# Attention stage: sample values of two pages ahead of the 256-column scores, and the head norm's small VectorE work behind a block's softmax difference

## Chip, cores and metric

One NeuronCore of one Trainium2 chip. The metric is the device time of the whole program in microseconds (us), the median of three runs. "TensorE" is PE in the profile (PEld is its weight load), VectorE is DVE, ScalarE is ACT, GpSimd is POOL, SyncE is SP.

## What is computed

One inference step of a two-layer decoder, all in float32: a Conformer-convolution layer and a differential-attention layer, each with a SwiGLU FFN behind it. The change lies in the attention layer, for 512 prompt tokens and 8 samples of 8 new tokens with 512 cached keys and values in 4 pages each; there are 8 heads.

```python
def diff_weights(scores, q_pos, k_pos, rel_bias, lam):
...
    logits = jnp.where((dist >= 0)[None, None, None], logits, -jnp.inf)
    p = jax.nn.softmax(logits, axis=-1)
    return p[:, :, 0] - lam * p[:, :, 1]
...
def attn_out(o, g, w, lam_init):
    B, T = o.shape[0], o.shape[1]
    o = rms_norm(o, g) * (1.0 - lam_init)
    return o.reshape(B, T, V_WIDTH) @ w
```

`o` is, for each head, the difference of two softmaxes times the values; it is RMS-normed over the head's 128 values ("head norm" below).

## The kernel before

Everything but attention is matmuls with split float32 operands. Attention is written as closures that are put into a plan by `at(round, rank, f)`; `play` runs the rounds in order and the closures of a round by rank. Each engine's instructions stand in the order in which they are written (class `InOrder`), so the plan sets the order on every engine's queue.

Each head takes four rounds. `prompt` handles its four blocks of 128 query rows as (3), (2) and (1, 0): `scores` (TensorE into the two banks `bS`, then on VectorE a custom bias-and-max instruction for each of the two softmaxes, and the exponentials with their sums on ScalarE), one round later `differ` (VectorE: RECIPROCAL, TENSOR_SCALAR and SCALAR_TENSOR_TENSOR, which waits for the sums of the exponentials) and `turn` (TensorE transposes, from the tile `pt`), and then `values`. Block (2) has score rows of 384 columns, blocks (1, 0) of 256 and 128.

`prompt_out` is the head norm: `squares`, then `power`, which on VectorE takes a RECIPROCAL and a TENSOR_REDUCE (the sums of squares), two TENSOR_TENSOR and a TENSOR_SCALAR on 128x4 elements, and on GpSimd raises four columns to the power -0.5 (the pow instruction, `sm<-sm,mhalf 128x4`). `scale` follows on VectorE: one 128x4 TENSOR_TENSOR that reads the result of pow, and the 128x512 multiplication into `t`; then `turn` and `low`. For head h the stages `scores` of the next head's block (2) and `power` stand in the same round.

`prepare_low` has GpSimd make the low parts of the queries and keys of a later head: two 128x512 subtractions, `whi<-xlo,whi` and `wlo<-xhi,wlo`, which wait for two casts of `prepare` on ScalarE. On GpSimd's queue they stand directly behind the pow of a head. The last two rounds with the norm of head 6 have no `prepare_low`; there `w_o_weights` has GpSimd make the low parts of the output projection's weights (`wlo<-raw,whi`) instead.

`sample` does the same for one sample and all heads: `scores` (q against the pages, `raw,qz`), `exponent`, `norm` and `combine`, `values` (32-column matmuls `raw,aTs` for pages 0 to 3 and `vv,aTs` for the new tokens), `power`, `scale`, `turn`. Near the end of attention `early` fills TensorE with the first matmuls of the output projection.

Of the kernel before, what the change touches and what calls it, by code (L numbers as in the profile page):

```python
# [36 lines left out]
def build(tc, A, O):  # L37
# [3 lines left out]
    with ctx:  # L41
# [35 lines left out]
        def tt():  # L77
            return tmp.tile([128, 640], F32, name="t")

        def sm(n=8):  # L80
            t = small.tile([128, 16], F32, name="sm")
            return t[:, :n]
# [195 lines left out]
        class Factors:  # L278
# [7 lines left out]
            def sums(self, i):  # L286
                return self.thi[:, i], self.tlo[:, i]
# [324 lines left out]
        with tc.tile_pool(name="h0", bufs=1) as hp0:  # L612
# [29 lines left out]
            with tc.tile_pool(name="cv", bufs=1) as cvp:  # L642
                c = cvp.tile([128, KT, T], F32, name="c")
                smid = Stats()
                with tc.tile_pool(name="u", bufs=2) as up:
# [146 lines left out]
                    r = smid.tok_half(0)  # L792
# [18 lines left out]
                    for i, (k, hf) in enumerate(steps):  # L811
# [5 lines left out]
                        if i == 0:  # L817
                            r = smid.tok_half(1)
# [38 lines left out]
        with tc.tile_pool(name="kvq", bufs=1) as kp:  # L857
# [164 lines left out]
            with tc.tile_pool(name="att", bufs=2) as ap_:  # L1022
                pages, slots = {}, {}

                def load_pages(src, b):
                    t = wp.tile([128, 4096], F32, name="raw", bufs=2)
                    for j in range(4):
                        if (b, j) not in slots:
                            slots[b, j] = nc.sync.value_load(pt[0:1, 4 * b + j:4 * b + j + 1], min_val=0, max_val=39)
                        r = slots[b, j]  # L1030
                        nc.sync.dma_start(out=t[:, j * 1024:(j + 1) * 1024],
                                          in_=A[src][bass.ds(r, 1)].rearrange("o p n -> p (o n)"))
                    pages[src, b] = t.rearrange("p (j h n) -> p j h n", j=4, h=8)
# [4 lines left out]
                def next_turn():  # L1038
                    turns[0] += 1
                    return bT[turns[0] % 2]  # L1040
# [4 lines left out]
                def at(r, rank, f):  # L1045
                    plan.setdefault(r, []).append((rank, f))

                def sample(b, r):
                    st_ = {}
# [45 lines left out]
                    def pov():  # L1095
                        return bP[:, :256].rearrange("p (g e) -> p g e", g=2)

                    def values(ks):
                        V, aT = pages["cv", b], st_["aT"]
                        for k in ks:  # L1100
                            for j in range(4):
                                if k < 4:
                                    l, r_ = aT[:, k, 16 * j:16 * j + 32], V[:, k, 2 * j:2 * j + 2, :]
                                else:
                                    l = aT[:64, k, 16 * j:16 * j + 32]
                                    r_ = vv[:64, 4, 256 * j:256 * j + 256].rearrange("p (g e) -> p g e", g=2)
                                pe.matmul(pov()[32 * j:32 * j + 32], lhsT=l, rhs=r_, start=(k == 0), stop=(k == 4))
                        if 4 in ks:
                            if b < 7:
                                load_pages("cv", b + 1)  # L1110
                            sq = st_["sq"] = tt()
                            ac.activation(out=sq[:, :256], in_=bP[:, :256], func=AF.Square)
# [37 lines left out]
                    at(r + 1, 0.2, norm)  # L1150
                    at(r + 1, 4, combine)
                    at(r + 2, 4, lambda: values((0, 1)))
                    at(r + 3, 2.47, lambda: values((2, 3, 4)))
                    at(r + 4, 1.9, power)
                    at(r + 5, 0.1, scale)
                    at(r + 5, 2.2, turn)
# [89 lines left out]
                def prompt_out(X, r):  # L1246
                    st_ = {}


                    def squares():  # L1250
                        pr = next_turn()[:, :4]
                        pe.matmul(pr, lhsT=rev, rhs=X.s0[:, :4], start=True, stop=True)
                        sq = st_["sq"] = tt()
                        ac.activation(out=sq[:, :512], in_=X.po, func=AF.Square)
                        st_["pr"] = pr

                    def power():
                        ss, r0 = sm(), sm()
                        st_["r0"] = r0
                        ve.reciprocal(out=r0[:, :4], in_=st_["pr"])  # L1260
                        ve.tensor_reduce(out=ss[:, :4], in_=st_["sq"][:, :512].rearrange("p (i e) -> p i e", i=4),
                                         axis=AX.X, op=ALU.add)
                        ve.tensor_tensor(out=ss[:, :4], in0=ss[:, :4], in1=r0[:, :4], op=ALU.mult)
                        ve.tensor_tensor(out=ss[:, :4], in0=ss[:, :4], in1=r0[:, :4], op=ALU.mult)
                        ve.tensor_scalar(out=ss[:, 4:8], in0=ss[:, :4], scalar1=1.0 / 128, scalar2=EPS,
                                         op0=ALU.mult, op1=ALU.add)
                        sc = st_["sc"] = sm()
                        po_.tensor_tensor(out=sc[:, :4], in0=ss[:, 4:8], in1=mhalf[:, :4], op=ALU.pow)

                    def scale():  # L1270
                        sc, r0 = st_["sc"], st_["r0"]
                        ve.tensor_tensor(out=sc[:, 4:8], in0=sc[:, :4], in1=r0[:, :4], op=ALU.mult)
                        on = st_["on"] = tt()
                        ve.tensor_tensor(
                            out=on[:, :512].rearrange("p (i e) -> p i e", i=4),
                            in0=X.po.rearrange("p (i e) -> p i e", i=4),
                            in1=sc[:, 4:8].rearrange("p (i o) -> p i o", o=1).broadcast_to([128, 4, 128]),
                            op=ALU.mult)

                    def turn():  # L1280
                        pT = X.po
                        for i in range(4):
                            pe.transpose(out=pT[:, i * 128:(i + 1) * 128], in_=st_["on"][:, i * 128:(i + 1) * 128],
                                         identity=ident)
                        ac.activation(out=xhi[:, X.h, :TP], in_=pT, func=AF.Copy, scale=gsub)

                    def low():
                        ve.scalar_tensor_tensor(out=xlo[:, X.h, :TP], in0=X.po, scalar=gsub,
                                                in1=xhi[:, X.h, :TP].bitcast(F32), op0=ALU.mult, op1=ALU.subtract)

                    at(r, 6, squares)
                    at(r + 1, 2.5, power)
                    q = 0 if X.last else 1
                    at(r + 1 + q, 2.3 if q else 7, scale)
                    at(r + 2 + q, 2.48 if q else 5, turn)
                    at(*((r + 4, 2.5) if q else (r + 2, 6)), low)


                for h_ in range(H):
                    X = Head()  # L1300
                    X.last = h_ == H - 1
                    r = 4 * h_ + 1
                    sample(h_, r - 1)
                    at(max(r - 3, 0), 6 if h_ else 0, lambda X=X, h_=h_: prepare(X, h_))
                    at(max(r - 1, 0), 0.1, lambda X=X: prepare_low(X))
                    prompt(X, (3,), r)
                    prompt(X, (2,), r + 1)
                    prompt(X, (1, 0), r + 2)
                    prompt_out(X, r + 4)
# [197 lines left out]
```

## Time and profile before

| | us |
|---|---|
| median of 3 runs | 1344.92 (1343.82 to 1345.35) |
| the profiled execution's own time | 1345.44 |
| its span, first to last instruction | 1343.7 |
| PE busy | 1327.9 (99%) |
| DVE busy | 918.1 (68%) |
| ACT busy | 599.2 (45%) |
| POOL busy | 117.9 (9%) |

Busy times count an instruction from its start to its end; PE's ends are modelled, so a busy PE can hold waits. All instructions of the kernel carry one line, L62, because a helper issues them; groups are told apart by the tiles. The attention stage lies from about 784 to 901 us, and repeats every 13.6 us, once for each head.

### The profile page before, as it was taken

How to read it: one execution, taken by the hardware profiler on the slowest of the kernel's cores; microseconds unless marked ns; L12 is line 12 of the kernel's file. 1: busy time of each engine (PE TensorE's matmuls, PEld its weight loads, DVE VectorE, ACT ScalarE, POOL GpSimd, SP SyncE). 2: the span in 40 equal slices, each digit the busy share in tenths (PEclk: the TensorE clock that was granted, in tenths of full speed). 3: DMA queues.
4: the chain of work that ended last, by engine and by line, in shares of the span. 5: the costliest groups of instructions: out<-in, count | busy, mean ns of one | idle time of the engine just before them, and what ended most of it. 6: DMA issues, size and time to landing. Idle time of an engine off the chain costs nothing.

```text
span 1343.7 us, 25259 instructions
## 1 busy us (share of the span) xinstructions
PE 1327.9 (99%) x10320; PEld 1225.1 (91%) x10320; DVE 918.1 (68%) x1803; ACT 599.2 (45%) x1224; POOL 117.9 (9%) x112
## 2 busy tenths in 40 slices
PE   8999999999999999999999999999999999999998
PEld 7988499999999999998787766689999999999998
DVE  6999375798658747764555258876679856865862
ACT  5122363345525524543454357764435533543550
POOL 0001112000000000011223113232100000000000
PEclk9999999999999999999999999999999999999999
DMA  8655412131321231252224178964021331231121
GB/s 307 203 170 167 108 66 93 32 126 64 123 98 64 95 126 64 88 208 91 79 98 160 63 267 322 343 232 156 32 94 64 110 111 63 105 116 63 63 95 71
DMA packets 57398, 168.00 MB, mean 125 GB/s; under 512 B 5970, under 2 KB 12754, under 8 KB 57154
## 3 DMA queue, kind: packets, MB, share of 16 engines
q1 hardware_dynamic: 55552, 163.85, 34.9%
q10 hardware_dynamic: 1730, 2.54, 0.6%
q8 instruction: 81, 1.33, 0.4%
q14 instruction: 35, 0.29, 0.1%
HBM read 145.56 MB, written 10.56 MB: 116 GB/s over the span
## 4 chain that ended last, share of the span: by engine, by line
PE 82%; DVE 13%; ACT 3%; DMA 1%; issue 1%; SPq 0%; POOL 0%; DVEq 0%; ACTq 0%
PE ps L62 82%; DVE c L62 5%; DVE xlo L62 2%; DVE wlo L62 2%; DVE t L62 2%; ACT xhi L62 1%; ACT t L62 1%; DVE u L62 1%; DMA up<-u 1%; DVE xhi L62 0%; DMA h<-in_xT 0%; ACT L62 0%; SPq L62 0%; DMA c_vec<-in_vec 0%; POOL sm L62 0%
## 5 line engine op out<-in xcount | busy, mean ns | idle before, releaser
L62 PE MATMUL ps<-xhi,whi 128*128 128x288 f32 x1776 | 414.1, 298 | 9.1 <-ACT xhi L62 8.4
L62 PE MATMUL ps<-xhi,wlo 128*128 128x288 f32 x1648 | 394.2, 296 | 0.0
L62 PE MATMUL ps<-xlo,whi 128*128 128x288 f32 x1520 | 367.4, 297 | 0.6 <-DVE xlo L62 0.5
L62 ACT CAST whi<-raw 128x512 fp32r<-128x512 f32 (+2 forms) x425 | 242.6, 593 | 155.2 <-PE ps L62 100.3
L62 PEld LDWEIGHTS ps<-xhi,whi 128*128 128x128 f32 x1776 | 296.4, 189 | 13.0 <-ACT xhi L62 9.2
L62 DVE TENSOR_TENSOR wlo<-raw,whi 128x512 fp32r<-128x512 f32 (+2 forms) x421 | 283.1, 690 | 26.8 <-ACT whi L62 25.8
L62 PEld LDWEIGHTS ps<-xhi,wlo 128*128 128x128 f32 x1648 | 278.9, 189 | 0.0
L62 PEld LDWEIGHTS ps<-xlo,whi 128*128 128x128 f32 x1520 | 258.6, 189 | 2.1 <-DVE xlo L62 1.9
L62 PE MATMUL ps<-xhiu,whi 128*128 128x288 f32 x832 | 224.7, 295 | 0.0
L62 PE MATMUL ps<-xlou,whi 128*128 128x288 f32 x832 | 224.6, 295 | 0.0
L62 PE MATMUL ps<-xhiu,wlo 128*128 128x288 f32 x832 | 224.0, 294 | 0.0
L62 PEld LDWEIGHTS ps<-xhiu,whi 128*128 128x128 f32 x832 | 149.2, 188 | 0.2
L62 PEld LDWEIGHTS ps<-xlou,whi 128*128 128x128 f32 x832 | 149.3, 188 | 0.0
L62 PEld LDWEIGHTS ps<-xhiu,wlo 128*128 128x128 f32 x832 | 149.2, 188 | 0.0
L62 DVE TENSOR_TENSOR t<-ps,t 128x288 f32<-128x288 f32 x172 | 75.1, 452 | 56.6 <-PE ps L62 45.7
L62 DVE TENSOR_TENSOR h<-ps,h 128x288 f32<-128x288 f32 x112 | 45.9, 451 | 71.6 <-PE ps L62 71.6
L62 DVE TENSOR_TENSOR t<-t 128x576 f32<-128x576 f32 (+1 forms) x53 | 39.6, 747 | 57.1 <-ACT t L62 56.1
L62 PE MATMUL ps<-whi,xhi 128*128 128x512 f32 x192 | 76.5, 398 | 0.0
L62 PE MATMUL ps<-wlo,xhi 128*128 128x512 f32 x192 | 76.0, 396 | 0.0
L62 PE MATMUL ps<-whi,xlo 128*128 128x512 f32 x192 | 75.8, 395 | 0.0
L62 DVE TENSOR_TENSOR raw<-raw 128x512 f32<-128x512 f32 x108 | 74.1, 686 | 1.2
L62 ACT COPY t<-ps 128x288 f32<-128x288 f32 x114 | 45.3, 397 | 46.0 <-PE ps L62 45.9
(144 smaller groups left out, 1421.0 us busy)
## 6 DMA issues: line engine op xcount, KB each, us to landing
raw<-in_w_gu SPq DMA_DIRECT2D x22, 2048.0 KB, 7.6
raw<-in_w_dn SPq DMA_DIRECT2D x12, 1536.0 KB, 6.5
raw<-in_ck SPq DMA_DIRECT2D x32, 512.0 KB, 7.3
raw<-in_cv SPq DMA_DIRECT2D x32, 512.0 KB, 5.8
raw<-in_w_kvq SPq DMA_DIRECT2D x6, 2048.0 KB, 9.0
raw<-in_w SPq DMA_DIRECT2D x5, 2048.0 KB, 8.4
up<-u SPq DMA_DIRECT2D x20, 270.0 KB, 4.3
us<-u SPq DMA_DIRECT2D x32, 144.0 KB, 4.0
```

The costliest lines, as they stand in the source:

```text
L62: r = f(*a, **k)
```

## The change

In `sample`, the values of pages 2 and 3 move from rank 2.47 to rank 1.9 of their round, in front of `scores` at rank 2; the values of the new tokens stay. In `prompt_out`, `power` is cut in two: `sums` (reciprocal and sums of squares) stays, and the rest moves to the next round at rank 0.05, behind `differ` at rank 0; for the last head it stays where it was.

```diff
                     at(r + 2, 4, lambda: values((0, 1)))
-                    at(r + 3, 2.47, lambda: values((2, 3, 4)))
+                    at(r + 3, 1.9, lambda: values((2, 3)))
+                    at(r + 3, 2.47, lambda: values((4,)))
...
-                    def power():
+                    def sums():
                         ss, r0 = sm(), sm()
-                        st_["r0"] = r0
+                        st_["r0"], st_["ss"] = r0, ss
                         ve.reciprocal(out=r0[:, :4], in_=st_["pr"])
                         ve.tensor_reduce(out=ss[:, :4], in_=st_["sq"][:, :512].rearrange("p (i e) -> p i e", i=4),
                                          axis=AX.X, op=ALU.add)
+
+                    def power():
+                        ss, r0 = st_["ss"], st_["r0"]
                         ve.tensor_tensor(out=ss[:, :4], in0=ss[:, :4], in1=r0[:, :4], op=ALU.mult)
...
                     at(r, 6, squares)
-                    at(r + 1, 2.5, power)
+                    at(r + 1, 2.5, sums)
+                    at(*((r + 1, 2.6) if X.last else (r + 2, 0.05)), power)
```

On VectorE, in the round of head 0's norm (heads 1 to 6 are alike), `sm` being the small tiles and `pt` the exponentials of block (2):

```order
 L62 RECIPROCAL sm<-ps 128x4
 L62 TENSOR_REDUCE sm<-t 128x4
+L62 RECIPROCAL sm<-sm 128x1
+L62 TENSOR_SCALAR sm<-sm,nlam 128x1
+L62 SCALAR_TENSOR_TENSOR pt<-pt,sm 128x384
 L62 TENSOR_TENSOR sm<-sm 128x4 x2
 L62 TENSOR_SCALAR sm<-sm 128x4
-L62 RECIPROCAL sm<-sm 128x1
-L62 TENSOR_SCALAR sm<-sm,nlam 128x1
-L62 SCALAR_TENSOR_TENSOR pt<-pt,sm 128x384
 L62 ISA pt,sm<-ps,Tb 128x256
```

The three instructions of `differ` now stand in front of the three of `power`; the same instructions are issued. GpSimd's queue is the same as before for heads 0 to 5 (pow, then the two subtractions). For head 6, near the output projection's weights, it reads:

```order
 L62 TENSOR_TENSOR wlo<-xhi,wlo 128x512
 L62 TENSOR_TENSOR sm<-sm,mhalf 128x2
+L62 TENSOR_TENSOR wlo<-raw,whi 128x512 x2
 L62 TENSOR_TENSOR sm<-sm,mhalf 128x4
-L62 TENSOR_TENSOR wlo<-raw,whi 128x512 x4
+L62 TENSOR_TENSOR wlo<-raw,whi 128x512 x2
 L62 TENSOR_TENSOR sm<-sm,mhalf 128x2
```

The pow of head 6 now stands behind the first two weight subtractions. On TensorE, once for each of the eight samples:

```order
 L62 MATMUL ps<-raw,aTs 32x256 x8
 L62 MATMUL ps<-c_rev,pt 128x128 x4
+L62 MATMUL ps<-raw,aTs 32x256 x8
 L62 MATMUL ps<-wlo,whi 128x256 x6
 L62 MATMUL ps<-wlo,whi 128x128 x6
-L62 MATMUL ps<-raw,aTs 32x256 x8
 L62 MATMUL ps<-vv,aTs 32x256 x4
 L62 MATMUL ps<-c_rev,pt 128x128 x3
```

The eight matmuls of pages 2 and 3 (16 records in the trace) moved ahead of the twelve of the scores of blocks (1, 0). SP's queue of DMA issues is in the same order as before.

## Rows read from the trace of the kernel before

**Rows 1.** Busy time in one head's stretch: span, PE, PEld, DVE, ACT, POOL, clock.
```profile
816.60:830.20 13.60, 13.60 (x148) 9.10 (x144) 12.08 (x48) 9.93 (x29) 4.19 (x4) 1.00 0.89 336
```
**Rows 2.** Timeline of TensorE's weight loads: start, us, instruction, [idle before, releaser].
```profile
817.21 0.18 PEld L62 LDWEIGHTS ps<-wlo,whi 64*128 64x128 f32 x1 [0.17 <-DVE sm L62]
817.57 0.76 PEld L62 LDWEIGHTS ps<-wlo,whi 64*128 64x128 f32 x11 [0.18 <-DVE sm L62]
...
819.97 0.31 PEld L62 LDWEIGHTS ps<-c_rev,pt 128*128 128x128 f32 x3 [0.41 <-DVE pt L62]
```
**Rows 3.** Timeline of VectorE over one head.
```profile
814.95 0.16 DVE L62 RECIPROCAL sm<-sm 128x1 f32<-128x1 f32 x1 [0.37 <-ACT pt L62]
...
818.22 0.36 DVE L62 TENSOR_TENSOR sm<-sm 128x4 f32<-128x4 f32 x2
818.61 0.17 DVE L62 TENSOR_SCALAR sm<-sm 128x4 f32<-128x4 f32 x1
818.69 0.15 DVE L62 RECIPROCAL sm<-sm 128x1 f32<-128x1 f32 x1
...
819.19 0.62 DVE L62 SCALAR_TENSOR_TENSOR pt<-pt,sm 128x384 f32<-128x384 f32 x1
819.73 0.41 DVE L62 CUSTOM_DVE_ANT_0 pt<-ps,Tb 128x256 f32<-128x256 f32 x1
...
820.84 0.39 DVE L62 TENSOR_TENSOR sm<-sm 128x4 f32<-128x4 f32 x1
...
824.53 0.28 DVE L62 CUSTOM_DVE_ANT_0 t<-ps,nbias,sm 128x64 f32<-128x64 f32 x1
...
825.75 0.16 DVE L62 RECIPROCAL sm<-sm 128x1 f32<-128x1 f32 x1 [0.60 <-ACT t L62]
...
828.53 0.16 DVE L62 RECIPROCAL sm<-sm 128x1 f32<-128x1 f32 x1 [0.37 <-ACT pt L62]
```
**Rows 4.** Timeline of ScalarE over the same head.
```profile
818.20 0.19 ACT L62 ACTIVATION_READ_ACCUMULATOR pt<-pt,sm 128x1 f32 x1
...
824.85 0.78 ACT L62 ACTIVATE t<-t,sm 128x576 f32<-128x576 f32 x1
...
828.32 0.19 ACT L62 ACTIVATION_READ_ACCUMULATOR pt<-pt,sm 128x1 f32 x1
```
**Rows 5.** Timeline of GpSimd over the same head.
```profile
818.95 1.01 POOL L62 TENSOR_TENSOR sm<-sm,mhalf 128x4 f32<-128x4 f32 x1 [7.98 <-ACT aT L62]
819.93 1.28 POOL L62 TENSOR_TENSOR whi<-xlo,whi 128x512 fp32r<-128x512 f32 x1
```
**Rows 6.** VectorE groups from 800 to 880 us by shape: count | busy, mean ns.
```profile
L62 DVE TENSOR_TENSOR sm<-sm 128x4 f32<-128x4 f32 x18 | 4.3, 238 | 0.4
...
L62 DVE SCALAR_TENSOR_TENSOR pt<-pt,sm 128x512 f32<-128x512 f32 x6 | 4.5, 752 | 0.2
...
L62 DVE SCALAR_TENSOR_TENSOR pt<-pt,sm 128x384 f32<-128x384 f32 x6 | 3.7, 619 | 0.2
...
L62 DVE SCALAR_TENSOR_TENSOR pt<-pt,sm 128x256 f32<-128x256 f32 x6 | 2.9, 476 | 0.0
```
**Rows 7.** GpSimd and VectorE side by side in an earlier stage, timeline.
```profile
209.00 1.43 POOL L62 TENSOR_TENSOR t<-t 128x576 f32<-128x576 f32 x1 [5.31 <-ACT t L62]
...
209.06 1.92 DVE L62 TENSOR_TENSOR wlo<-raw,whi 128x512 fp32r<-128x512 f32 x1 [0.27 <-ACT whi L62]
```
**Rows 8.** Timeline of the last head: ScalarE, GpSimd, VectorE, TensorE.
```profile
886.73 1.14 ACT L62 CAST whi<-raw 128x512 fp32r<-128x512 f32 x2
...
887.90 2.52 POOL L62 TENSOR_TENSOR wlo<-raw,whi 128x512 fp32r<-128x512 f32 x2
...
891.59 0.97 DVE L62 TENSOR_SCALAR sm<-sm 128x2 f32<-128x2 f32 x1
...
894.46 0.42 DVE L62 TENSOR_TENSOR t<-ps,sm 128x256 f32<-128x256 f32 x1 [1.90 <-POOL sm L62]
...
895.46 0.38 PE L62 MATMUL ps<-c_ident,t 128*128 128x128 f32 x2
```

## The prediction, made before the change was run

> **What bounds the kernel now.** I first read the busy times, by slices and then for one head's stretch of the attention stage: TensorE counts as busy for all 13.60 us of 13.60, VectorE for 12.08, ScalarE for 9.93 [rows 1]. That looks like TensorE, but its ends are modelled, so I looked for the waits. In TensorE's weight loads there is one plain wait in the stretch that the change touches: the first load of the 256-column scores goes at 817.21, the other eleven at 817.57, 0.36 us later, released by VectorE's maxima of the block before, which free the second score bank [rows 2]. The transposes of block (2) at 819.97 are put down to `differ` (0.41), but that one ended at 819.19 + 0.62 = 819.81 [rows 2, 3], so TensorE's own previous work counts there too.
>
> Then I followed VectorE and ScalarE around one head. RECIPROCAL at 814.95 waits for a sum of exponentials. From there VectorE hardly pauses until the sample's last maximum at 824.53 + 0.28 = 824.81 [rows 3]; ScalarE starts the sample's exponential at 824.85 [rows 4]; VectorE's RECIPROCAL at 825.75 waits for it (0.60 idle); the next block's maxima and two exponentials follow, whose sum ends at 828.32 + 0.19 = 828.51, and RECIPROCAL at 828.53 waits for that [rows 3, 4]. From 814.95 to 828.53 is 13.58 us, the whole period, and no link in it is TensorE's. So the ring of VectorE and ScalarE sets the pace, and TensorE has at least the 0.36 us to spare.
>
> **The change, part by part.**
>
> *Values of two pages ahead of the scores.* The same matmuls and as many changes of tile shape, so no work is added; they cover the wait of 0.36 us. If TensorE were the bound, eight samples would give 8 x 0.36 = 2.9 us. It is not, so I put the gain at 0; the cover is the ring above, and if that had slack the gain would be the 2.9. The scores finish some 0.6 us later than now, at about 818.9 for the first bank; their maxima start at 819.73 now [rows 3] and later in the change, so nothing waits for them. No DMA moves: the pages' loads are issued behind the values of the new tokens, as now.
>
> *`differ` ahead of the small work.* Seven heads, 0 to 6. Now: two 4-column products at 818.22, TENSOR_SCALAR at 818.61, then RECIPROCAL at 818.69 and the difference at 819.19 [rows 3]. In the change RECIPROCAL must wait for the sum that ScalarE reads until 818.20 + 0.19 = 818.39 [rows 4]; with the 0.03 that other such waits take it starts at 818.42, 0.27 earlier than now, and the difference at 818.92. The small work starts 0.54 us behind that (819.73 - 819.19, the step to the next instruction), at 819.46, and its TENSOR_SCALAR ends 0.56 later (818.61 + 0.17 - 818.22), at 820.02. So VectorE idles about 0.20 us (it could go on at 818.22 before, at 818.42 now), the transposes get their operand 0.27 us earlier, and the pow gets its operand late.
>
> *The pow and what is queued behind it.* GpSimd starts the pow 0.17 us behind TENSOR_SCALAR (818.61 + 0.17 to 818.95). In the change that is 820.19, 1.24 us later than now. Behind it on the same queue stand the two 128x512 subtractions, ready long before; the first starts as the pow ends (819.93 against 818.95 + 1.01) and takes 1.28 [rows 5]. It would run from 821.17 to 822.45. Who waits for the pow is the first product of `scale`, a 4-column TENSOR_TENSOR on VectorE. Before, the pow was done when it came up at 820.84, and yet it took 0.39, ending at 821.23, 0.02 behind the end of the first subtraction (819.93 + 1.28 = 821.21) [rows 3, 5]. The 18 of this shape average 238 ns [rows 6], which fits twelve at 0.16 and six at 0.39: once a head the product is held until the subtraction has ended. The same shows elsewhere: with a GpSimd addition from 209.00 to 210.43, a VectorE subtraction that began at 209.06 took 1.92 [rows 7]. GpSimd's start only 0.06 us earlier was enough.
>
> In the change the product can start when the pow has signalled its end, and by then GpSimd has begun the subtraction (it starts 0.03 before the pow's record ends). So the product is held until 822.45 and ends at 822.47 instead of 821.23: 1.24 us later. All that follows on VectorE up to the sample's maximum is in the ring, so I count it in full: 6 heads (0 to 5) x 1.24 = 7.4 us. The 0.20 us of idle lies inside it. The bounds of this term: 0.20 a head if the hold does not occur (1.2 us), 1.24 + 1.28 if the product also misses the gap between the two subtractions (15.1 us).
>
> The Trainium skill, page "SBUF — State Buffer", section "Who interferes with whom", says that a VectorE instruction with two SBUF inputs contends with a GpSimd instruction that reads SBUF, and that the loser blocks for the whole instruction. On the subtractions the trace agrees (the 0.39 above). On the pow it does not: a difference with two SBUF inputs started at 819.19, within the pow, and took 0.62 [rows 3, 5], on the line of its neighbours of 256 and 512 columns at 476 and 752 ns against 619 [rows 6]. By the page it would have been held to 819.96, and freeing it would return up to 0.77 a head, making the term 6 x 0.47 = 2.8; by the row there is nothing to return, and the sum takes the row.
>
> *Head 6.* No `prepare_low` follows; the pow now stands behind two weight subtractions. Their casts run from 886.73, the first done at about 887.3 [rows 8], so GpSimd is ready at about 887.4, while VectorE is in the difference (818.92 to 819.54 in the head above, 67.97 us later here: 886.89 to 887.51). I expect GpSimd to take its turn at 887.51, and the small products behind the difference to be held through both subtractions, 2.52 us [rows 8], to 890.03; a TENSOR_SCALAR of this kind was held once already, 0.97 against 0.17 elsewhere [rows 3, 8]. VectorE's next maxima then start at about 890.2 instead of 887.70, 2.5 us late. The sample's last product, at 894.46 + 0.42 = 894.88, shifts as much, and TensorE's turn of it at 895.46 had 0.58 to spare [rows 8]: 1.9 us late. The final matmuls hang on that. Bounds: 0 if the products slip in first and the output projection's matmuls hide the rest, 2.5 if nothing hides.
>
> *Sum.* 7.4 + 1.9 = 9.3 us on the profiled execution's 1345.4 gives 1354.8 (span 1343.7 to 1353.0). That execution lies 0.5 above the median of 1344.9, so the forecast is **1354.3 us**, 0.7% slower.
>
> **Rivals.**
>
> *The hold does not bite* (VectorE's product gets in between pow and subtraction): 6 x 0.20 + 1.9 = 3.1, 1348.0 us. For it: how the two engines' requests are ordered within 0.05 us is not shown at this spot. Against it: 0.06 us decided for GpSimd in [rows 7].
>
> *TensorE is the bound after all*, the ring has slack that the trace hides, and the change does what its place suggests: -2.9, 1342.0 us, faster. It decides if VectorE's chain can slip by over 1.2 us a head unnoticed. For it: 13.60 of 13.60 busy [rows 1]. Against it: the closed ring of 13.58, with both its waits on ScalarE's sums [rows 3, 4].
>
> *The product misses the gap as well*: 15.1 + 1.9 = 17.0, 1361.9 us. Against it: in the six heads of before it got in at the end of the first subtraction each time (the mean of [rows 6] leaves no room for longer ones).
>
> **How the numbers follow.** The forecast has 0.74, with a range of its own of 1351 to 1355.5 (a head's 1.0 to 1.28, and 0 to 2.5 for head 6: 6.0 to 10.2, and a little for joints). The harmless hold has 0.14, TensorE as the bound 0.07, the missed gap 0.05. The range 1347.5 to 1356 takes in the forecast and most of the harmless hold, and leaves out some 0.15. A measurement here can tell about 0.2% (2.7 us) from no change: faster is below 1342.2, slower above 1347.6. TensorE as the bound gives faster 0.05 and same 0.02; the harmless hold lies near the upper border, 0.06 of it same; the rest, 0.87, is slower.
>
> **What would show it.** Right: in the heads 0 to 5 the period grows from 13.6 to some 14.8 us; the first product of `scale` waits for GpSimd and ends 0.02 us behind the first subtraction; pow starts about 1.2 us later in the period; the 0.36 us between the first and second weight load of the 256-column scores is gone, and TensorE waits elsewhere, above all in front of the 512-column scores, whose bank the sample's maxima free. In head 6 the small products take over a microsecond each. Wrong: a period of 13.6 or less, or a product of 0.16 us straight behind the pow. The sum fails if the ring has a slack that I read as dense work, or if the hold in head 6 falls the other way; the first would cost most of the 7.4, the second 1.9.

## The result, and the profile after

The changed kernel took 1353.32 us, the median of 5 runs (1352.35 to 1356.94), beside 1344.35 for the kernel before on the same chip (5 runs, 1343.05 to 1345.35): ratio 1.0072, 95% interval 1.0061 to 1.0082. It is slower, by 9.0 us where 9.3 were forecast. The profiled execution took 1354.38 us (forecast 1354.8), its span is 1352.6 (forecast 1353.0).

The page of the changed kernel, its span and the busy times:

```profile
span 1352.6 us, 25272 instructions
...
PE 1331.8 (98%) x10320; PEld 1226.4 (91%) x10320; DVE 925.0 (68%) x1803; ACT 599.0 (44%) x1224; POOL 117.9 (9%) x112
```

VectorE counts 6.9 us more than before with the same instructions: some of them got longer. One head's stretch, from one RECIPROCAL that waits for the 512-column sums to the next (columns as in [rows 1]):

```profile
816.09:830.88 14.79, 14.00 (x147) 9.10 (x146) 12.96 (x48) 9.93 (x30) 4.19 (x4) 1.00 0.79 294
```

The period is 14.79 us instead of 13.58. TensorE now shows 0.79 us of idle where it had none, so it is not what grew. VectorE's timeline over this head, to be laid beside [rows 3]:

```profile
816.09 0.16 DVE L62 RECIPROCAL sm<-sm 128x1 f32<-128x1 f32 x1 [0.37 <-ACT pt L62]
...
819.55 0.16 DVE L62 RECIPROCAL sm<-sm 128x1 f32<-128x1 f32 x1 [0.23 <-ACT pt L62]
...
820.06 0.62 DVE L62 SCALAR_TENSOR_TENSOR pt<-pt,sm 128x384 f32<-128x384 f32 x1
820.60 0.35 DVE L62 TENSOR_TENSOR sm<-sm 128x4 f32<-128x4 f32 x2
820.98 0.17 DVE L62 TENSOR_SCALAR sm<-sm 128x4 f32<-128x4 f32 x1
821.06 0.42 DVE L62 CUSTOM_DVE_ANT_0 pt<-ps,Tb 128x256 f32<-128x256 f32 x1
...
822.36 1.23 DVE L62 TENSOR_TENSOR sm<-sm 128x4 f32<-128x4 f32 x1
823.63 0.69 DVE L62 TENSOR_TENSOR t<-ps,sm 128x512 f32<-128x512 f32 x1
824.24 0.21 DVE L62 RECIPROCAL sm<-sm 128x1 f32<-128x1 f32 x2
824.43 0.46 DVE L62 TENSOR_SCALAR sm<-sm,nlam 128x1 f32<-128x1 f32 x2
824.80 0.74 DVE L62 SCALAR_TENSOR_TENSOR pt<-pt,sm 128x256 f32<-128x256 f32 x2
...
826.82 0.28 DVE L62 CUSTOM_DVE_ANT_0 t<-ps,nbias,sm 128x64 f32<-128x64 f32 x1
...
828.10 0.16 DVE L62 RECIPROCAL sm<-sm 128x1 f32<-128x1 f32 x1 [0.66 <-ACT t L62]
...
830.88 0.16 DVE L62 RECIPROCAL sm<-sm 128x1 f32<-128x1 f32 x1 [0.37 <-ACT pt L62]
```

GpSimd over the same head, to be laid beside [rows 5]:

```profile
821.32 1.01 POOL L62 TENSOR_TENSOR sm<-sm,mhalf 128x4 f32<-128x4 f32 x1 [9.20 <-PE ps L62]
822.30 1.28 POOL L62 TENSOR_TENSOR whi<-xlo,whi 128x512 fp32r<-128x512 f32 x1
823.54 1.27 POOL L62 TENSOR_TENSOR wlo<-xhi,wlo 128x512 fp32r<-128x512 f32 x1
```

The pow starts 5.23 us into the period (821.32 - 816.09) instead of 4.00 (818.95 - 814.95). The four-column product was free to go at 822.36, 0.06 us behind the start of the first subtraction, and ends at 823.59, 0.01 behind that subtraction's end (822.30 + 1.28): 1.23 us for an instruction of 0.16. All six heads show this, at 1.231 to 1.236 us.

The starts of the first 512-column maxima give the sum by heads. Before they lie 14.48, 13.59, 13.59, 13.60, 13.59, 13.60 and 13.61 us apart, after 14.62, 14.81, 14.79, 14.79, 14.80, 14.80 and 14.80: 7.4 us over seven steps, of which 0.14 are in the first. From the last of them to the start of the last transpose of head 7's result it is 20.40 us before (880.58 to 900.98) and 22.13 after (887.74 to 909.87): 1.7 us. The attention stage begins 0.2 us earlier, so the span grows by 8.9.

TensorE's weight loads, to be laid beside [rows 2]: the 256- and 128-column scores go in one piece of twelve, and a new wait stands in front of the 512-column scores.

```profile
819.35 0.77 PEld L62 LDWEIGHTS ps<-wlo,whi 64*128 64x128 f32 x12 [0.41 <-DVE sm L62]
...
826.72 0.18 PEld L62 LDWEIGHTS ps<-wlo,whi 64*128 64x128 f32 x1 [0.93 <-DVE sm L62]
```

Head 6, VectorE and then GpSimd, to be laid beside [rows 8]:

```profile
894.59 1.31 DVE L62 TENSOR_TENSOR sm<-sm 128x4 f32<-128x4 f32 x2
895.94 1.21 DVE L62 TENSOR_SCALAR sm<-sm 128x4 f32<-128x4 f32 x1
897.06 0.41 DVE L62 CUSTOM_DVE_ANT_0 pt<-ps,Tb 128x256 f32<-128x256 f32 x1
```

```profile
894.58 2.54 POOL L62 TENSOR_TENSOR wlo<-raw,whi 128x512 fp32r<-128x512 f32 x2 [8.47 <-ACT whi L62]
897.29 1.01 POOL L62 TENSOR_TENSOR sm<-sm,mhalf 128x4 f32<-128x4 f32 x1 [0.17 <-DVE sm L62]
```

The two products and the TENSOR_SCALAR take 2.56 us, up to 897.15; 897.12 is the end of the second weight subtraction.

### The profile page after: what moved, and what is told of

Its sections match the earlier page's. It is cut to its first block, busy times and chain, and to the rows that moved or that the text cites. A ratio compares the mean times of both kernels' runs of the same rounds, so it can differ in the third digit from the quotient of the medians.

```text
span 1352.6 us, 25272 instructions
## 1 busy us (share of the span) xinstructions
PE 1331.8 (98%) x10320; PEld 1226.4 (91%) x10320; DVE 925.0 (68%) x1803; ACT 599.0 (44%) x1224; POOL 117.9 (9%) x112
## 4 chain that ended last, share of the span: by engine, by line
PE 79%; DVE 15%; ACT 3%; DMA 1%; issue 1%; POOL 1%; SPq 0%; DVEq 0%; ACTq 0%
PE ps L62 79%; DVE c L62 5%; DVE t L62 3%; DVE xlo L62 2%; DVE wlo L62 2%; DVE sm L62 1%; ACT xhi L62 1%; ACT t L62 1%; POOL sm L62 1%; DVE u L62 1%; DVE pt L62 1%; DMA up<-u 0%; DVE xhi L62 0%; DMA h<-in_xT 0%; ACT pt L62 0%
```

## The experiments

Two theories stood against each other. **Ring**: VectorE and ScalarE set the pace; the late pow puts GpSimd's subtraction in front of VectorE's product, and that is the loss. **TensorE**: TensorE's stream sets the pace, and its order, or its waits for score banks, is what the change altered. Times are medians, with the ratio to runs of the kernel before on the same chip; "period" is the step between the heads' first 512-column maxima.

**The change in halves.** `e1_values_only`, before with the first half of the diff:

```diff
-                    at(r + 3, 2.47, lambda: values((2, 3, 4)))
+                    at(r + 3, 1.9, lambda: values((2, 3)))
+                    at(r + 3, 2.47, lambda: values((4,)))
```

> The kernel before with the values of pages 2 and 3 moved alone. Ring theory (VectorE and ScalarE set the period): the 0.36 us between the first and second weight load of the 256-column scores goes, the period stays 13.59 us, the time within 0.1% of before (1343 to 1345.5). Rival (TensorE is the bound): 0.36 a sample, period 13.2, about 1341.5, 0.2% faster. Rival (the move itself costs): period over 13.7.

1345.08 us, ratio 1.0002 (0.9993 to 1.0011), period 13.59. The first step grew from 14.48 to 14.63, as in the changed kernel. The scores go in one piece of twelve weight loads there (from 818.57), and TensorE idles 0.18 us in front of the next transposes instead (to 820.23), for VectorE's difference. Filling TensorE's wait is worth nothing.

`e2_power_only`, the changed kernel with `values((2, 3, 4))` back at rank 2.47:

> The kernel before with the head norm's small work moved behind the difference alone. Ring theory: all of the change's loss is here: period 14.8 us in the heads 0 to 5, product of scale 1.23 us, some 9 us above before (1353.3, ratio 1.0066 +- 0.001). Rival (the two moves add up or hamper each other): under 6 us or over 11 us above before.

1353.82 us, ratio 1.0072 (1.0058 to 1.0086), period 14.80. The move of `power` is the whole loss.

**The subtractions taken away.** `e3_after_no_sub` is the changed kernel, `e4_before_no_sub` the kernel before, each without the two subtractions of heads 2 to 7: the low parts of these heads' queries and keys are not computed, the high parts stand in for them.

```diff
                 def prepare_low(X):
+                    if X.h >= 2:
+                        for t2, src in X.parts:
+                            t2[1] = t2[0]
+                        return
```

> The changed kernel without the two GpSimd subtractions behind the pow (for heads 2 to 7 the high parts stand in for the low parts of queries and keys, so the low parts' share of the scores is left out; all matmuls stay). Hold theory: with nothing on GpSimd behind the pow the product takes 0.16 us; only the wait for the late pow and the idle of 0.20 stay: period about 13.8 us, total 2.5 to 4 us above before (1347 to 1348.5). Rival (the lateness of the pow or the order itself is the cost, not the subtraction): period 14.5 or more, 1352 or more.

1348.15 us, ratio 1.0029 (1.0018 to 1.0039), period 13.86. VectorE and GpSimd of `e3_after_no_sub`:

```profile
821.37 0.16 DVE L62 TENSOR_TENSOR sm<-sm 128x4 f32<-128x4 f32 x1
...
822.18 0.41 DVE L62 RECIPROCAL sm<-sm 128x1 f32<-128x1 f32 x2
```

```profile
820.33 1.01 POOL L62 TENSOR_TENSOR sm<-sm,mhalf 128x4 f32<-128x4 f32 x1 [9.20 <-PE ps L62]
```

The pow is as late as in the changed kernel, and the product goes 0.03 us behind its end and takes 0.16. Of the 1.21 us a head, 0.94 belong to the hold (14.80 - 13.86) and 0.27 to the new order. The 0.27 are not VectorE's wait for the late pow, 0.11 us in front of 821.37: ScalarE's exponentials end later still, since the second RECIPROCAL waits for their sum (the pair lasts 0.41). 0.20 of them is the idle in front of the 384-column difference, by which the 256-column maxima come later in the period (4.98 us into it against 4.78), and 0.07 lies between the sample's last maximum and the RECIPROCAL that waits for its exponential (1.29 against 1.22).

> The kernel before without the same two subtractions (the same share of the scores left out). Hold theory: the product falls from 0.39 to 0.16 us, the period from 13.59 to about 13.36, six heads give 1.4 us: 1342.9. Rival (no hold in the kernel before): period 13.59, 1344.3.

1345.45 us, ratio 1.0005 (0.9996 to 1.0014), period 13.60: no gain, against the expectation. VectorE of `e4_before_no_sub` shows where it went:

```profile
821.00 0.42 DVE L62 CUSTOM_DVE_ANT_0 pt<-ps,Tb 128x256 f32<-128x256 f32 x1
...
822.11 0.16 DVE L62 TENSOR_TENSOR sm<-sm 128x4 f32<-128x4 f32 x1
822.30 0.69 DVE L62 TENSOR_TENSOR t<-ps,sm 128x512 f32<-128x512 f32 x1
...
823.36 0.16 DVE L62 RECIPROCAL sm<-sm 128x1 f32<-128x1 f32 x1 [0.29 <-ACT pt L62]
```

The product is down to 0.16 as expected, and then the RECIPROCAL of block (0) idles 0.29 us for ScalarE: ScalarE reads its last sum from 823.14 to 823.32. ScalarE runs four exponentials after the first 256-column maxima, and from these to that RECIPROCAL it is 2.36 us (823.36 - 821.00). So there are two branches between the two points, one through VectorE's product and multiplication and one through ScalarE. In the kernel before they end within 0.1 us of each other. VectorE and then ScalarE of the kernel before, in that place:

```profile
821.87 0.37 DVE L62 RECIPROCAL sm<-sm 128x1 f32<-128x1 f32 x2
822.16 0.44 DVE L62 TENSOR_SCALAR sm<-sm,nlam 128x1 f32<-128x1 f32 x2
```

```profile
821.86 0.19 ACT L62 ACTIVATION_READ_ACCUMULATOR pt<-pt,sm 128x1 f32 x1
```

The pair of RECIPROCALs lasts 0.37 us where back to back it lasts 0.21 (changed kernel, at 824.24): the second waits for the sum that ScalarE has at 822.05.

**VectorE relieved without leaving work out.** `e6_product_pool`, before with the product on GpSimd:

```diff
                         po_.tensor_tensor(out=sc[:, :4], in0=ss[:, 4:8], in1=mhalf[:, :4], op=ALU.pow)
+                        po_.tensor_tensor(out=sc[:, 4:8], in0=sc[:, :4], in1=r0[:, :4], op=ALU.mult)
...
-                        ve.tensor_tensor(out=sc[:, 4:8], in0=sc[:, :4], in1=r0[:, :4], op=ALU.mult)
```

> The kernel before with the 4-column product of scale issued on GpSimd right behind the pow instead of on VectorE. Ring theory: VectorE goes straight on to the 512-column multiplication, which reads PSUM and was not held by the subtractions: 0.43 us a head less in the ring, period 13.16 us, if TensorE can follow; total 2.6 to 3.0 us below before (1341.6). Rival (TensorE is just behind the ring): period 13.3 to 13.5, under 2 us below. Rival (ring is wrong): 13.59.

1345.68 us, ratio 1.0008 (0.9999 to 1.0017), period 13.66: a miss, for the reason just told. VectorE waits 0.49 us at the RECIPROCAL:

```profile
823.35 0.16 DVE L62 RECIPROCAL sm<-sm 128x1 f32<-128x1 f32 x1 [0.49 <-ACT pt L62]
```

The 0.07 by which the period is longer lie behind the sample's last maximum, as in `e3_after_no_sub`.

`e7_fold` takes VectorE's small work of the norm from six instructions to two, the 512-column multiplication aside (ScalarE squares the sum of exponentials, and the pow's result needs no further factor); `e8_fold_values` has the values move as well:

```diff
+                        ac.activation(out=r0[:, :4], in_=pr, func=AF.Square, scale=EPS ** 0.5)
...
-                        ve.reciprocal(out=r0[:, :4], in_=st_["pr"])
-                        ve.tensor_tensor(out=ss[:, :4], in0=ss[:, :4], in1=r0[:, :4], op=ALU.mult)
-                        ve.tensor_tensor(out=ss[:, :4], in0=ss[:, :4], in1=r0[:, :4], op=ALU.mult)
-                        ve.tensor_scalar(out=ss[:, 4:8], in0=ss[:, :4], scalar1=1.0 / 128, scalar2=EPS,
-                                         op0=ALU.mult, op1=ALU.add)
+                        ve.scalar_tensor_tensor(out=ss[:, 4:8], in0=ss[:, :4], scalar=1.0 / 128, in1=r0[:, :4],
+                                                op0=ALU.mult, op1=ALU.add)
...
-                        ve.tensor_tensor(out=sc[:, 4:8], in0=sc[:, :4], in1=r0[:, :4], op=ALU.mult)
```

> The kernel before with the head norm rewritten: the squared sum of exponentials times EPS is taken on ScalarE, one SCALAR_TENSOR_TENSOR adds the mean of squares, and the pow gives the final factor; RECIPROCAL, two products, TENSOR_SCALAR and the product of scale go. Ring theory: 0.27 us less before the difference (up to ScalarE's sum) and 0.43 less in scale, 0.70 a head, period 12.9 us if TensorE follows; TensorE without the wait of 0.36 needs some 13.15 to 13.2 and still has that wait, so I expect a period of 13.1 to 13.3, 2.5 to 4 us below before (1340.5 to 1342). Ring wrong: 13.59.

> The same with the values of pages 2 and 3 moved ahead of the 256-column scores as in the change. Ring theory: now TensorE's wait counts, since VectorE is no longer the slowest: period 12.9 to 13.1 us, 0.1 to 0.3 below the kernel without the move, in all 3.5 to 4.8 us below before (1339.5 to 1341). Rival (the move gives nothing there either): the same time as without it.

1344.19 us (0.9987 to 1.0005) and 1343.98 us (0.9988 to 1.0006): no difference that can be measured. The periods did fall, to 13.43 and 13.39, by 0.16 and 0.20 instead of 0.3 to 0.5 and 0.5 to 0.7: what stands behind the 256-column maxima is again cut off by ScalarE's four exponentials. VectorE of `e7_fold`:

```profile
819.74 0.42 DVE L62 CUSTOM_DVE_ANT_0 pt<-ps,Tb 128x256 f32<-128x256 f32 x1
...
822.10 0.16 DVE L62 RECIPROCAL sm<-sm 128x1 f32<-128x1 f32 x1 [0.49 <-ACT pt L62]
```

It is 2.36 us again (822.10 - 819.74). The 0.27 us ahead of the maxima are gained (they come 4.51 us into the period, 4.78 before), and 0.10 of them is lost again between the sample's last maximum and its RECIPROCAL (1.32 us against 1.22).

**The two branches put to the test.** An extra multiplication of 256 columns in that stretch, in the kernel before (`e9_before_extra`) and in `e7_fold`, the folded one (`e10_fold_extra`); the first half of the result is written twice (in the folded kernel with the pow's own columns, `sc[:, 0:2]`):

```diff
+                        ve.tensor_tensor(
+                            out=on[:, :256].rearrange("p (i e) -> p i e", i=2),
+                            in0=X.po[:, :256].rearrange("p (i e) -> p i e", i=2),
+                            in1=sc[:, 4:6].rearrange("p (i o) -> p i o", o=1).broadcast_to([128, 2, 128]),
+                            op=ALU.mult)
                         ve.tensor_tensor(
                             out=on[:, :512].rearrange("p (i e) -> p i e", i=4),
```

> Before, with a second VectorE multiplication of 256 columns (the first half of the head norm's result, written and then written again) ahead of the 512-column one, that is in the stretch between the 256-column maxima and the RECIPROCAL of blocks (1, 0), in which ScalarE's four exponentials take 2.36 us. If VectorE and ScalarE end that stretch together (theory), the extra step of about 0.35 us a head is paid but for 0.03: period 13.59 to 13.91, some 2.3 us in all, 1346.9. If TensorE sets the pace (rival), VectorE has room: period 13.59, 1344.6.

> The folded head norm (e7_fold) with the same extra multiplication of 256 columns. There VectorE waits 0.49 us for ScalarE's sum at the end of that stretch, so by the theory the extra 0.35 us is free: period 13.43 as in e7_fold, 1344.2. If VectorE's own work were the pace there, it would cost 0.35 a head: 13.78, 1346.7.

`e9_before_extra`: 1347.17 us, ratio 1.0021 (1.0011 to 1.0030), period 13.97. VectorE of it:

```profile
822.27 1.15 DVE L62 TENSOR_TENSOR t<-ps,sm 128x256 f32<-128x256 f32 x2
```

The extra step takes 0.46 us (1.15 for the pair, 0.69 for the second alone), and 0.38 of it is paid. So VectorE's branch has no more than some 0.1 us of slack. TensorE, with the same work, goes at 13.43 in `e7_fold`, and is not the pace of the kernel before. `e10_fold_extra`: 1345.44 us, ratio 1.0004 (0.9995 to 1.0013), a time that does not decide; its period is 13.42 to 13.43 in four of the six steps behind the first, as in `e7_fold`, so there the same instruction is free. The other two are longer (13.58 and 14.22). In both, the scores against a sample's cached keys start as the load of a page of keys lands: at 808.27 and 835.83, behind landings at 808.13 and 835.63. In the latter TensorE's weight loads stand idle for 0.81 us, which the view puts down to VectorE; the load took 9.86 us from issue to landing, 8.48 in `e7_fold`. In the kernel before, each page has landed 0.69 us or more ahead of these scores, and 0.93 or more in the changed one, so the loads set the pace in neither.

**The hold alone.** `e11_after_product_pool` is the changed kernel with the product on GpSimd, between pow and subtraction (the diff of `e6_product_pool`).

> After, with the four-column product of scale on GpSimd, between the pow and the first subtraction. The late pow stays, the hold of VectorE's product goes. If the hold is the larger part of the loss (theory): the 512-column multiplication starts some 0.3 us behind the pow's end, 0.95 us a head earlier than in after; period 14.79 to 13.84, time 1347.6. If lateness of the pow alone, or TensorE's order, is the cause (rival): period stays near 14.8 and the time near 1353.

1354.95 us, ratio 1.0077 (1.0063 to 1.0091), period 14.88: no gain. That number is the one given for the rival, but the trace shows another cause. VectorE and GpSimd of `e11_after_product_pool`:

```profile
822.24 0.69 DVE L62 TENSOR_TENSOR t<-ps,sm 128x512 f32<-128x512 f32 x1 [0.39 <-POOL sm L62]
...
823.09 0.44 DVE L62 TENSOR_SCALAR sm<-sm,nlam 128x1 f32<-128x1 f32 x2
823.45 1.76 DVE L62 SCALAR_TENSOR_TENSOR pt<-pt,sm 128x256 f32<-128x256 f32 x2
```

```profile
820.92 1.01 POOL L62 TENSOR_TENSOR sm<-sm,mhalf 128x4 f32<-128x4 f32 x1 [9.28 <-PE ps L62]
822.00 0.20 POOL L62 TENSOR_TENSOR sm<-sm 128x4 f32<-128x4 f32 x1
822.15 1.28 POOL L62 TENSOR_TENSOR whi<-xlo,whi 128x512 fp32r<-128x512 f32 x1
823.40 1.26 POOL L62 TENSOR_TENSOR wlo<-xhi,wlo 128x512 fp32r<-128x512 f32 x1
```

The multiplication starts 0.31 us behind the pow's end, as expected, and VectorE is 0.93 us earlier in the period than in the changed kernel at the TENSOR_SCALARs. Then the difference of block (1), two SBUF inputs, comes up 0.05 us behind the start of the second subtraction, and the pair of differences takes 1.76 us instead of 0.74. The hold moved to the next instruction that it applies to.

**The wait for ScalarE filled.** `e12_fold_values_split` is `e8_fold_values` with `differ` block by block:

```diff
                             ve.reciprocal(out=m[:, 3:4], in_=m[:, 2:3])
-                        for i in blocks:
-                            t, m = st_[i]
                             ve.tensor_scalar(out=m[:, 4:5], in0=X.s0[:, i:i + 1], scalar1=nlam, scalar2=m[:, 3:4],
                                              op0=ALU.mult, op1=ALU.mult)
-                        for i in blocks:
-                            t, m = st_[i]
                             ve.scalar_tensor_tensor(out=t[:, 0, :], in0=t[:, 1, :], scalar=m[:, 4:5],
```

> The folded head norm with the values move (e8_fold_values), with differ written block by block, so that block 1's TENSOR_SCALAR and difference stand ahead of the RECIPROCAL of block 0 that waits 0.49 us for ScalarE. If the ring of VectorE and ScalarE is still the pace at 13.39 us: some 0.11 us a head less, 13.28, 1343.2. If TensorE's own stream is the pace by then (its gaps in e8_fold_values are those of tile changes alone): 13.39 as in e8_fold_values, 1344.0.

1344.13 us, ratio 0.9995 (0.9986 to 1.0004), period 13.48, worse than the 13.39 of `e8_fold_values`. VectorE and GpSimd:

```profile
821.51 0.64 DVE L62 SCALAR_TENSOR_TENSOR pt<-pt,sm 128x256 f32<-128x256 f32 x1
```

```profile
820.59 1.27 POOL L62 TENSOR_TENSOR wlo<-xhi,wlo 128x512 fp32r<-128x512 f32 x1
```

The early difference ran into the subtraction and took 0.64 instead of 0.48 [rows 6]; it ends 0.28 us behind the subtraction, as the one of `e11_after_product_pool` does (1.50 of the 1.76, ending at 824.95 against 824.66). Once more the period moved with VectorE's order, so VectorE's branch has no slack at 13.39; whether TensorE has any there is not shown.

**The head without subtractions.** `e5_head6_old`, the changed kernel with head 6's `power` in its old place:

```diff
-                    at(*((r + 1, 2.6) if X.last else (r + 2, 0.05)), power)
+                    at(*((r + 1, 2.6) if X.last or r == 29 else (r + 2, 0.05)), power)
```

> The changed kernel with head 6's small work left in its old place. Theory: the heads 0 to 5 keep their period of 14.8 us; head 6 loses the 2.3 us in which its small products wait for the weight subtractions, of which 1.7 reached the end: 1351.6, 7.2 us above before. Rival (what head 6 lost was hidden by the output projection's matmuls): the same as the changed kernel, 1353.3.

1352.37 us, ratio 1.0060 (1.0046 to 1.0073). From the last 512-column maxima to the start of the last transpose it is 20.30 us (886.94 to 907.24) instead of 22.13: head 6's share is 1.8 us.

No version here is faster than the kernel before by more than 0.2%.

## Why the prediction was right

**The values move: 0 forecast, none measured**, by `e1_values_only`. It adds 0.14 us once, in the first step, which the prediction did not see; the scores are one piece, as foreseen, and nothing follows from it.

**Heads 0 to 5: 7.4 us forecast, 7.2 measured** (7.4 over seven steps, less the 0.14). Each link came as told: the pow 1.23 us later in the period (forecast 1.24), the subtraction behind it, the product held until its end. VectorE's idle in front of the 384-column difference is 0.23, forecast 0.20.

One thing was read wrongly, and it almost cancelled, by luck: the prediction counted the 1.24 in full because VectorE "hardly pauses" in the ring. In the kernel before, VectorE was not the later branch in that stretch; ScalarE's four exponentials were, by 0.10 us. So the first RECIPROCAL behind the multiplication comes 1.23 us later in the period (8.15 against 6.92), and the TENSOR_SCALARs only 1.13 (8.34 against 7.21). Later 0.06 comes back: from the sample's last maximum to the RECIPROCAL that waits for its exponential it is 1.28 us (828.10 - 826.82) instead of 1.22 [rows 3]. 1.23 - 0.10 + 0.06 = 1.19, of 1.21 measured.

The same misreading is why the expectations of `e4_before_no_sub` and `e6_product_pool` failed and those of `e7_fold` and `e8_fold_values` were too large. They took the 0.39 us of the product in the kernel before [rows 3] for a cost that could be had back. A delay of 1.2 us goes through two branches that end together almost in full; a relief of 0.2 to 0.4 us on one of them gives nothing.

**Head 6: 1.9 forecast, 1.7 measured** (1.8 by `e5_head6_old`). The forecast had the small products held through both subtractions, 2.52 us. They were, with one difference: the pair took 1.31, so the first product slipped in at about its own 0.15, the second ended with the first subtraction, and the TENSOR_SCALAR with the second.

**The rivals.** That the hold does not bite is refuted by six products of 1.23 us; its price was 1348.0, and `e3_after_no_sub`, where nothing is there to hold in the heads 0 to 5, measured 1348.15. TensorE as the bound is refuted by `e1_values_only`, and by `e9_before_extra` beside `e7_fold`. A product that misses the gap as well did not occur.

**The rule on SBUF.** The Trainium skill, page "SBUF — State Buffer", section "Who interferes with whom", says which VectorE instructions contend with a reading GpSimd instruction: those with two SBUF inputs, and some with one, TENSOR_SCALAR among them where its operands allow a mode with two ports; not one with at most one SBUF input otherwise. The traces agree on the subtractions: held were TENSOR_TENSOR and SCALAR_TENSOR_TENSOR from SBUF and the four-column TENSOR_SCALAR (1.23, 1.50 and 1.21 us), and not held the 512-column multiplication out of PSUM within a subtraction (0.69 at 823.63), nor two TENSOR_SCALARs of one column (0.46 at 824.43).

**What stays open.** In `e8_fold_values` the heads are 0.20 us shorter, some 1.4 us in all, and the median of the runs is only 0.6 lower, within what can be measured. The stretch of lower clock told below would account for it, but it is seen only in profiles, one for each kernel, and the mean granted clock of the single runs does not order their times: of the runs of `e8_fold_values`, one at 1.00 took 1342.73 us, four at 0.999 took 1342.38 to 1344.61, five at 0.998 took 1342.86 to 1345.11, and one at 0.997 took 1348.03.

## What to carry to other kernels

Moving a small instruction also moves what stands behind its consumer on another queue: the small instructions that moved cost little where they now stand; what cost was the subtraction that their lateness put in front of a four-column product. Before a piece of a ring is called its cost, look for a second branch between the same two points: if an engine's last instruction there ends within a tenth of a microsecond of the other's, making one shorter gains nothing, and making one longer is paid. And a held instruction taken away exposes the next one of its kind: check what comes up within the rest of the other engine's work.

## What the runs showed of the hardware

Not expected: a difference of 128x256 that came up only 0.05 us behind the start of a GpSimd subtraction was held for all of it, 1.50 us for 0.48; the kernel before misses this by 0.06 to 0.08 us in six heads (in the head shown the second subtraction runs from 821.17 to 822.45, and the difference starts at 822.51).

ScalarE starts the sample's exponential 0.04 us behind the last maximum in the kernel before (824.85 against 824.81, [rows 3, 4]) and 0.10 us behind it in the changed one (827.20 against 827.10). How long ScalarE stood idle does not decide it: in `e6_product_pool` its previous instruction had ended 0.02 us ahead of the maximum's end, and it is 0.10; in `e9_before_extra` that was 0.40 us, and it is 0.04. What does decide it is not shown.

The granted clock of TensorE fell to half, 1.2 GHz, for 3.4 us in some profiles. From 167.9 to 171.3 us in the changed kernel no cost shows, since the attention stage began no later. In `e11_after_product_pool` it fell from 887.9 to 891.3 us, behind the periods compared above. Between 1004 and 1011 us it did cost, in the profiles of `e7_fold`, `e8_fold_values`, `e10_fold_extra` and `e12_fold_values_split`: from the last transpose of attention to the end they take 444.5 us, the kernel before and the changed one 442.7. The stretch of 15 us there, first in the kernel before, then in `e8_fold_values` (columns as in [rows 1]):

```profile
1000.00:1015.00 15.00, 13.64 (x101) 13.16 (x100) 13.38 (x26) 6.35 (x11) 0.00 (x0) 1.00 0.58 214
```

```profile
1000.00:1015.00 15.00, 13.33 (x87) 12.86 (x86) 14.09 (x28) 5.22 (x10) 0.00 (x0) 0.89 0.41 156
```

TensorE gets 87 matmuls done instead of 101, at a mean granted clock of 0.89. In `e8_fold_values` it is idle for 1.67 us of these 15 (15.00 - 13.33), all of it in the three microseconds before the fall, and for as much in the other three with the fall; the kernel before is idle for 1.36 us (15.00 - 13.64) and keeps its clock. Why the four with the folded norm stand idle longer there, no run here shows.
